# A hybrid decoder layer: key bias by DMA broadcast in place of six-row matmuls, and one new lane item per batch

## The chip, the core and the metric

The kernel runs on one core of a Trainium2 chip. The metric is the device time of one execution in microseconds (us). The core has a matrix engine (TensorE, PE in the profile; its weight loads are listed as PEld), a vector engine (VectorE, DVE), a scalar engine (ScalarE, ACT), GpSimd (POOL) and a queue engine (SyncE, SP). Each engine works through its own list of instructions in order; semaphores order them between engines.

## What is computed

One layer on 256 tokens of width 2048: a half-step feed-forward layer, a mixing layer of three attention groups, a second half-step feed-forward layer. All of it is float32 at the interface.

```python
x = x + 0.5 * swiglu(rms_norm(x, ffn1_norm), ffn1_gate, ffn1_up, ffn1_down)     # 2048 -> 5632 -> 2048
h = rms_norm(x, mix_norm); proj = h @ w_in
fq, fk, fv, f_logit, sq, sk, sv, mq = split(proj)
# A: forgetting attention, 6 heads of 128
log_f = log_sigmoid(f_logit + forget_bias); c = cumsum(log_f, axis=sequence)
s = (rms(fq) @ rms(fk).T) * scale + c[query] - c[key];  s = where(key <= query, s, NEG_INF)
out_a = softmax(s) @ fv
# B: windowed attention (128), 6 query heads on 2 key heads, distance penalty, sink logit
# C: 4 heads of attention into 256 memory rows
x = x + concat(out_a, out_b, out_c) @ w_out
x = x + 0.5 * swiglu(rms_norm(x, ffn2_norm), ffn2_gate, ffn2_up, ffn2_down)
```

The term that the change is about is `- c[key]`, one number for each key and each head, the same for all queries.

## The kernel before

**Projections and batches.** Every weight matrix goes through `project`. A batch is two slices of 128 rows of the weight, 512 columns wide (384 or 390 in parts of `w_in`). `load_w` issues its DMA on SP (tag `raw`, four buffers), ScalarE rounds it to a high part (`hi`, L205, three buffers), VectorE subtracts to get the low part (`lo`, L206, three buffers). `mm_rows` then runs three matmuls for each half of the tokens and each slice: high by high (L248), high activations by low weights (L249), low by high (L250). So a batch is 12 matmuls, and a projection of `w_in` has 8 batches. After each batch, `project` calls `lanes.tick()` once.

**Side work between batches.** Everything else is cut into stages, Python generators, which `Lanes` runs between the batches. A generator issues the instructions of a stage and yields the number of batches until its next stage. There are two kinds. Items given to `lanes.run` start at the next tick. Items given to `lanes.put` wait in a queue until those that they name have ended, and then until one of two lanes is free; each lane has its own PSUM tile (tags `l0`, `l1`). In `tick` both lanes may take a new item in the same call. `finish` calls `tick` without a projection batch until the named items have ended. The framework's planner may shift instructions on an engine among neighbours, but TensorE's order follows the code here.

**The mixing layer.** Its chunks of `w_in` come in the order mq, sqa (with the six forget logits), skv, sqb, fqa, fka, fqb, fkb, fva, fvb. After each, `heads_T` normalises the heads: squares of each head and token half on ScalarE (L396, 8 for four heads, 6 for three), reciprocal root on VectorE, scaled copies on ScalarE, transposes on TensorE back into the chunk's accumulator (L412), one copy out. Its stages lie 1, 3, 2 and 1 batches apart. The accumulators have two buffers.

`forget` makes the cumulative sums with small matmuls: `cq` for queries (128 partitions) and the negated `nck` for keys, on six partitions, one for each head (L481). It is put after sqa; in the profile `nck` is written during batch 7 of sqb.

`logits` handles a pair of heads: a windowed pair (w0, w2, w4) has four query-key matmuls (L495), two for each head, of 128 and 256 columns. A forgetting pair (f0, f2, f4) has before each of them a matmul that adds `nck` to every row of the tile: its weights are one sixth of `sel`, six rows of 128, a selector with ones in row h for head h (L493). Three batches later VectorE adds `cq` and the causal mask `cmask` from PSUM to SBUF (L507), takes the maxima, and three batches on ScalarE takes the exponentials. A float32 matmul is listed as two records in the profile.

f0 starts after batch 7 of fqb; f2 and f4 become ready together and start in both lanes after the last batch of fva.

## Time and profile before

| | |
|---|---|
| median of 3 runs | 1846.38 us (1846.11 to 1847.82) |
| the profiled execution | 1845.47 us |
| its span, first to last instruction | 1843.7 us |
| TensorE's mean granted clock in the span | 0.998 |
| busy: TensorE, weight loads, VectorE, ScalarE, GpSimd | 1829.9, 1538.8, 938.9, 846.4, 11.1 us |
| moved by DMA | 343.36 MB, mean 186 GB/s |

Busy is the time in which an engine works on an instruction, and matmuls overlap each other in these records, so the busy time of TensorE is no measure of how full it is; the distance between the starts of two matmuls is. Times in the rows are from the span's start. A granted clock of 1.00 is 2.4 GHz, 0.50 is 1.2 GHz. All rows come from the one profiled execution.

### The profile page before, as it was taken

How to read it: one execution, taken by the hardware profiler on the slowest of the kernel's cores; microseconds unless marked ns; L12 is line 12 of the kernel's file. 1: busy time of each engine (PE TensorE's matmuls, PEld its weight loads, DVE VectorE, ACT ScalarE, POOL GpSimd, SP SyncE). 2: the span in 40 equal slices, each digit the busy share in tenths (PEclk: the TensorE clock that was granted, in tenths of full speed). 3: DMA queues.
4: the chain of work that ended last, by engine and by line, in shares of the span. 5: the costliest groups of instructions: out<-in, count | busy, mean ns of one | idle time of the engine just before them, and what ended most of it. 6: DMA issues, size and time to landing. Idle time of an engine off the chain costs nothing.

```text
span 1843.7 us, 21918 instructions
## 1 busy us (share of the span) xinstructions
PE 1829.9 (99%) x8448; PEld 1538.8 (83%) x8448; DVE 938.9 (51%) x1121; ACT 846.4 (46%) x1148; POOL 11.1 (1%) x31
## 2 busy tenths in 40 slices
PE   8999999999999999999999999999999999999998
PEld 6888888888888888888998888888888888888887
DVE  5554544555445554645655455555555454544443
ACT  6444444444435443656665455444444444433332
POOL 2000000000000000000000000000000000000000
PEclk9999999999999999999999999999999999999999
DMA  7666666666656566565555556666666666666663
GB/s 231 192 189 189 193 186 191 191 188 192 187 191 206 194 210 193 176 175 147 161 143 145 179 181 189 192 186 192 188 190 193 184 192 187 192 194 204 206 204 128
DMA packets 182520, 343.36 MB, mean 186 GB/s; under 512 B 11088, under 2 KB 28048, under 8 KB 182416
## 3 DMA queue, kind: packets, MB, share of 16 engines
q1 hardware_dynamic: 180368, 339.04, 61.6%
q10 hardware_dynamic: 1696, 2.89, 0.4%
q8 instruction: 66, 1.08, 0.3%
q14 instruction: 38, 0.31, 0.1%
q0 software_dynamic: 352, 0.03, 0.0%
HBM read 339.83 MB, written 2.10 MB: 185 GB/s over the span
## 4 chain that ended last, share of the span: by engine, by line
PE 97%; DMA 1%; ACT 1%; DVE 1%; issue 0%; DVEq 0%; ACTq 0%
PE ga L248 4%; PE ga L250 4%; PE ga L249 4%; PE ua L248 4%; PE gb L248 4%; PE db L249 4%; PE db L250 4%; PE gb L249 4%; PE gb L250 4%; PE ub L248 4%; PE ua L249 4%; PE ua L250 4%; PE ub L249 4%; PE ub L250 4%; PE db L248 4%; PE da L249 4%
## 5 line engine op out<-in xcount | busy, mean ns | idle before, releaser
L206 DVE TENSOR_TENSOR lo_bu<-raw_bu,hi_bu 128x1024 fp32r<-128x1024 f32 x88 | 107.8, 1225 | 131.5 <-ACT hi_bu L205 131.5
L206 DVE TENSOR_TENSOR lo_au<-raw_au,hi_au 128x1024 fp32r<-128x1024 f32 x88 | 107.8, 1225 | 130.1 <-ACT hi_au L205 130.1
L206 DVE TENSOR_TENSOR lo_bd<-raw_bd,hi_bd 128x1024 fp32r<-128x1024 f32 x88 | 107.7, 1224 | 124.0 <-ACT hi_bd L205 124.0
L206 DVE TENSOR_TENSOR lo_ad<-raw_ad,hi_ad 128x1024 fp32r<-128x1024 f32 x88 | 107.8, 1224 | 119.5 <-ACT hi_ad L205 119.5
L205 ACT CAST hi_bd<-raw_bd 128x1024 fp32r<-128x1024 f32 x88 | 92.8, 1055 | 145.0 <-PE db L250 139.8
L206 DVE TENSOR_TENSOR lo_ag<-raw_ag,hi_ag 128x1024 fp32r<-128x1024 f32 x88 | 108.1, 1229 | 98.7 <-ACT hi_ag L205 98.7
L206 DVE TENSOR_TENSOR lo_bg<-raw_bg,hi_bg 128x1024 fp32r<-128x1024 f32 x88 | 107.7, 1223 | 99.2 <-ACT hi_bg L205 99.2
L205 ACT CAST hi_ad<-raw_ad 128x1024 fp32r<-128x1024 f32 x88 | 92.7, 1053 | 131.5 <-PE da L250 106.4
L205 ACT CAST hi_bg<-raw_bg 128x1024 fp32r<-128x1024 f32 x88 | 92.7, 1054 | 127.2 <-PE gb L250 68.3
L205 ACT CAST hi_ag<-raw_ag 128x1024 fp32r<-128x1024 f32 x88 | 92.7, 1054 | 122.5 <-PE ga L250 66.3
L205 ACT CAST hi_bu<-raw_bu 128x1024 fp32r<-128x1024 f32 x88 | 92.7, 1054 | 115.5 <-PE ub L250 79.0
L205 ACT CAST hi_au<-raw_au 128x1024 fp32r<-128x1024 f32 x88 | 92.7, 1054 | 115.3 <-PE ua L250 79.4
L248 PE MATMUL ga<-hi_ag,x0T 128*128 128x512 f32 x352 | 138.7, 394 | 0.0
L248 PE MATMUL gb<-hi_bg,x2T 128*128 128x512 f32 x352 | 137.9, 392 | 0.0
L250 PE MATMUL ga<-hi_ag,x0T 128*128 128x512 f32 x352 | 137.3, 390 | 0.0
L249 PE MATMUL ga<-lo_ag,x0T 128*128 128x512 f32 x352 | 137.3, 390 | 0.0
L248 PE MATMUL da<-hi_ad,hT_a 128*128 128x512 f32 x352 | 137.2, 390 | 0.0
L249 PE MATMUL da<-lo_ad,hT_a 128*128 128x512 f32 x352 | 137.1, 389 | 0.1
L250 PE MATMUL gb<-hi_bg,x2T 128*128 128x512 f32 x352 | 137.1, 389 | 0.0
L248 PE MATMUL ua<-hi_au,x0T 128*128 128x512 f32 x352 | 137.0, 389 | 0.0
L248 PE MATMUL db<-hi_bd,hT_b 128*128 128x512 f32 x352 | 137.0, 389 | 0.0
L249 PE MATMUL gb<-lo_bg,x2T 128*128 128x512 f32 x352 | 137.0, 389 | 0.0
(460 smaller groups left out, 3959.7 us busy)
## 6 DMA issues: line engine op xcount, KB each, us to landing
raw_ag<-in_ffn_gate_dram SPq DMA_DIRECT2D x88, 512.0 KB, 4.5
raw_au<-in_ffn_up_dram SPq DMA_DIRECT2D x88, 512.0 KB, 3.7
raw_ad<-in_ffn_down_dram SPq DMA_DIRECT2D x88, 512.0 KB, 4.7
raw_bg<-in_ffn_gate_dram SPq DMA_DIRECT2D x88, 512.0 KB, 4.3
raw_bu<-in_ffn_up_dram SPq DMA_DIRECT2D x88, 512.0 KB, 3.7
raw_bd<-in_ffn_down_dram SPq DMA_DIRECT2D x88, 512.0 KB, 4.6
raw_wo<-in_w_out_dram SPq DMA_DIRECT2D x16, 512.0 KB, 3.7
raw_mk<-in_w_mem_k_dram SPq DMA_DIRECT2D x8, 512.0 KB, 3.8
```

The source lines that it names most:

```text
L205: nc.scalar.copy(h, r)
L206: nc.vector.tensor_tensor(out=l, in0=r, in1=h.bitcast(F32), op=ALU.subtract)
L248: nc.tensor.matmul(acc[:, t, :w], hi, wh, start=first, stop=False)
L249: nc.tensor.matmul(acc[:, t, :w], hi, wl, start=False, stop=False)
L250: nc.tensor.matmul(acc[:, t, :w], lo, wh, start=False, stop=last)
```

## The change

Three edits. First, the negated key sums are no longer added by matmuls. `nck` becomes a corner of a tile `nck_all` of 128 partitions by six heads by 384 keys. GpSimd's queue writes the six rows to a DRAM scratch tile and reads them back to all 128 partitions (six rows of 1.5 KB, 9 KB for each partition). `add_mask`, an item of its own, waits six batches and then adds the causal mask to one head in each batch. The forgetting logits wait for it, and L507 takes `nck_all` where it took `cmask`. The six-row matmuls, `sel` and its two instructions go. Second, in `tick` only one of the lanes may take a new item. Third, `heads_T` squares one half of the tokens, waits a batch, squares the other, and waits two batches before the copies where it waited three.

```diff
     def tick(self):
         self.free = [i for i in self.free if self._step(i)]
+        started = False
         for n in range(2):
-            if self.lane[n] is None:
+            if self.lane[n] is None and not started:
                 for q in self.queue:
                     if all(d in self.done for d in q[2]):
                         self.queue.remove(q)
                         self.lane[n] = [q[0], q[1](f"l{n}"), 0]
+                        started = True
                         break
...
+    dpool = ctx.enter_context(tc.tile_pool(name="scratch", bufs=1, space=bass.MemoryType.DRAM))
...
-    sel = cpool.tile([6, 6, P], F32, name="sel")
...
-        nc.gpsimd.memset(sel, 0.0)
-        nc.gpsimd.affine_select(out=sel, in_=sel, compare_op=ALU.not_equal, fill=1.0, base=0,
-                                pattern=[[-1, 6], [0, P]], channel_multiplier=1)
...
                     nc.scalar.activation(junk, acc[:, t, cols(h)], AF.Square, scale=r[:, t:t + 1],
                                          accum_out=s[:, t, h:h + 1])
-            yield 1
+                yield 1
...
-            yield 3
+            yield 2
...
-        nck = mx.tile([6, 3 * P], F32, name="nck")
+        nck_all = mx.tile([P, 6, 3 * P], F32, name="nck_all")
+        nck = nck_all[0:6, 0, :]
+        nck_dram = dpool.tile([6, 3 * P], F32, name="nck_dram")
...
+        def add_mask():
+            yield 6
+            for h in range(6):
+                nc.vector.tensor_tensor(out=nck_all[:, h, :], in0=nck_all[:, h, :], in1=cmask, op=ALU.add)
+                yield 1
...
+            nc.gpsimd.dma_start(nck_dram, nck)
+            nc.gpsimd.dma_start(nck_all.rearrange("p h s -> p (h s)"),
+                              nck_dram.rearrange("h s -> (h s)")[None, :].to_broadcast([P, 6 * 3 * P]))
+            lanes.run("mask", add_mask())
...
                 for t, keys in enumerate((k[:, 0:P], k)):
-                    if fox:
-                        nc.tensor.matmul(sp[:, i, SEG[t]], sel[:, h0 + i, :], nck[:, SEG[t]], start=True,
-                                         stop=False)
-                    nc.tensor.matmul(sp[:, i, SEG[t]], q[:, t * P:(t + 1) * P], keys, start=not fox,
-                                     stop=True)
+                    nc.tensor.matmul(sp[:, i, SEG[t]], q[:, t * P:(t + 1) * P], keys, start=True, stop=True)
...
-                            in1=cmask[:, SEG[t]], op0=ALU.add, op1=ALU.add)
+                            in1=nck_all[:, h0 + i, SEG[t]], op0=ALU.add, op1=ALU.add)
...
-                lanes.put("f0", fox_logits(0), ("forget", "fqa", "fka"))
+                lanes.put("f0", fox_logits(0), ("mask", "fqa", "fka"))
...
-                    lanes.put(f"f{h}", fox_logits(h), ("forget", "fqa", "fka", "fqb", "fkb"))
+                    lanes.put(f"f{h}", fox_logits(h), ("mask", "fqa", "fka", "fqb", "fkb"))
```

## Rows read from the trace of the kernel before

**Rows 1.** The page, first section: engine, busy us, share, instructions.
```profile
PE 1829.9 (99%) x8448; PEld 1538.8 (83%) x8448; DVE 938.9 (51%) x1121; ACT 846.4 (46%) x1148; POOL 11.1 (1%) x31
```

**Rows 2.** TensorE's waits, 100 to 1840: us in total, times, longest.
```profile
PE sqa L249 <- DVE lo_sqa L206: 0.5, 1, 0.5
```

**Rows 3.** Windows: stretch, its us, busy us by engine, PEclk, DMA share, GB/s.
```profile
885.00:890.00 5.00, 5.00 (x31) 4.90 (x30) 3.48 (x12) 4.37 (x15) 0.00 (x0) 1.00 0.17 48
985.00:992.00 7.00, 7.00 (x32) 4.36 (x30) 2.87 (x7) 2.14 (x4) 0.00 (x0) 1.00 0.57 164
992.00:999.00 7.00, 7.00 (x19) 5.07 (x19) 2.95 (x9) 2.12 (x9) 0.00 (x0) 0.51 0.01 2
```

**Rows 4.** TensorE's timeline around f0: start us, duration us, what, idle before.
```profile
944.63 0.34 PE L250 MATMUL fqb<-hi_fqb,x1T 128*128 128x384 f32 x1
944.90 0.48 PE L493 MATMUL s_f<-nck,sel 6*128 6x128 f32 x2
...
949.16 0.33 PE L249 MATMUL fkb<-lo_fkb,x1T 128*128 128x384 f32 x1
```

**Rows 5.** TensorE's timeline around w0, and six ordinary steps after it.
```profile
884.77 0.33 PE L250 MATMUL sqb<-hi_sqb,x1T 128*128 128x384 f32 x1
884.94 1.47 PE L495 MATMUL s_w<-qkv 128*128 128x128 f32 x8
...
886.43 0.34 PE L249 MATMUL fqa<-lo_fqa,x1T 128*128 128x384 f32 x1
...
887.47 0.33 PE L249 MATMUL fqa<-lo_fqa,x1T 128*128 128x384 f32 x1
```

**Rows 6.** TensorE's timeline around f2 and f4.
```profile
986.09 0.34 PE L250 MATMUL fva<-hi_fva,x1T 128*128 128x384 f32 x1
...
991.99 1.22 PE L495 MATMUL s_f<-qkv 128*128 128x256 f32 x2
...
996.39 0.88 PE L248 MATMUL fvb<-hi_fvb,x1T 128*128 128x384 f32 x1
...
998.92 0.34 PE L249 MATMUL fvb<-lo_fvb,x1T 128*128 128x384 f32 x1
```

**Rows 7.** TensorE's timeline around v0 with v2, and around v4.
```profile
1029.14 0.39 PE L250 MATMUL wo<-hi_wo0e,mixT 128*128 128x512 f32 x1
...
1032.22 0.40 PE L249 MATMUL wo<-lo_wo1e,mixT 128*128 128x512 f32 x1
...
1039.94 0.39 PE L250 MATMUL wo<-hi_wo1e,mixT 128*128 128x512 f32 x1
...
1041.70 0.40 PE L249 MATMUL wo<-lo_wo1e,mixT 128*128 128x512 f32 x1
```

**Rows 8.** Timelines of ScalarE and TensorE at the squares of `mq`.
```profile
816.49 0.37 ACT L396 ACTIVATE junkh<-mq,y_x 128x128 f32<-128x128 f32 x1 [1.87 <-PE mq L250]
...
819.25 2.36 ACT L205 CAST hi_sqa<-raw_sqa 128x780 fp32r<-128x780 f32 x3
...
821.38 0.44 PE L249 MATMUL sqa<-lo_sqa,x1T 128*128 128x390 f32 x1 [0.48 <-DVE lo_sqa L206]
```

**Rows 9.** DMA issues: tile, issuing queue, count, KB each, median us to landing.
```profile
raw_fqa<-in_w_in_dram SPq DMA_DIRECT2D x8, 384.0 KB, 4.2
x_sb<-in_x_dram ACTq DMA_DIRECT2D x3, 512.0 KB, 11.5
graw<-in_ffn_norm_dram POOLq DMA_DIRECT2D x1, 8.0 KB, 6.7
```

**Rows 10.** Timelines of VectorE and TensorE from the key bias to the last `fqa` batch.
```profile
883.01 0.54 DVE L481 TENSOR_SCALAR nck<-cps 6x384 f32<-6x384 f32 x1
886.52 1.02 DVE L512 SCALAR_TENSOR_TENSOR ss_w<-dist,s_w 128x384 f32<-128x384 f32 x2 [2.98 <-PE s_w L495]
...
897.77 0.96 DVE L206 TENSOR_TENSOR lo_fqa<-raw_fqa,hi_fqa 128x768 fp32r<-128x768 f32 x1 [0.41 <-ACT hi_fqa L205]
...
901.66 0.34 PE L249 MATMUL fqa<-lo_fqa,x1T 128*128 128x384 f32 x1
```

## The prediction

> **What bounds the kernel now.** I read the page first: TensorE is busy for 1829.9 us of a span of 1843.7 us, at a mean granted clock of 0.998 [rows 1]. Next the waits: between the start and the end TensorE waits once, for 0.5 us, on a `lo` tile of batch `sqa` [rows 2]. So an edit is worth what it takes from TensorE's own queue, or what new wait it puts there; ScalarE, VectorE and the DMA queues have time left. Then the windows around the forgetting attention's logits: from 985 to 992 the engine is busy 7.00 of 7.00 us at clock 1.00, from 992 to 999 busy 7.00 of 7.00 us at 0.51, which is the lower level of 1.2 GHz, and 19 matmuls go through where 32 went before [rows 3]. The clock fell there with no idle time ahead of it. Last, the timeline of TensorE by start times [rows 4 to 7]. A matmul's own duration overlaps the next one's, so I price an interlude between projection matmuls as the distance of two ordinary starts on either side of it, and compare interludes by these distances.
>
> **The six-row matmuls.** The change removes four per pair of heads, for three pairs. The pair f0 runs alone and at full clock: from the last L250 before it (944.63) to the L249 after it (949.16) there are 4.53 us, with four six-row and four query-key matmuls (two records each) in between [rows 4]. The windowed pair w0 has the same four query-key matmuls, 8 records of 128 and 256 columns, and no six-row ones: from 884.77 to 886.43, 1.66 us [rows 5]. After the change a forgetting pair has the form of w0. Saved for f0: 4.53 - 1.66 = 2.87 us.
>
> Pairs f2 and f4 start in one batch and stand back to back. From L250 at 986.09 to the eighth projection matmul after them, L249 at 998.92, there are 12.83 us [rows 6]. Six ordinary steps of 384 columns lie between the second and the eighth; w0's are 887.47 - 886.43 = 1.04 us, so 0.173 each [rows 5]. That leaves 12.83 - 1.04 = 11.79 us to the second one. After the change f4 starts one batch later, so there are two interludes like w0's: 1.66 for the first, and 1.66 less two ordinary steps, 1.31, for the second. Saved: 11.79 - 1.66 - 1.31 = 8.82 us. Of this the clock is 11.79 - 4.53 - (4.53 - 0.35) = 3.08 us, the rest is again 2.87 per pair. Sum of both places: 11.69 us.
>
> That counts the clock as staying up. My reason: it fell at 991.99, inside the longest run of such work in the trace, 10 us from the L250 at 986.09 to the L248 at 996.39 [rows 6], and not in f0's run of 4 us with the same matmuls [rows 4]; after the change such a run is w0's, 8 records in 1.47 us [rows 5], with a whole batch of 12 projection matmuls between f2 and f4.
>
> The row also says why so much goes: f0 costs 4.18 us beyond its ordinary steps and w0 1.31, so adding as many six-row matmuls more than triples the cost. The Trainium skill (TensorE: Matmul & The Clock Gate, section Why this matters for your kernels) says that a single matmul of few rows takes the same time as one of 128; by that each six-row matmul would cost what its query-key partner costs in w0, and the three pairs would be worth 3 x 1.31 = 3.9 us in place of 8.6. The trace disagrees where the two kinds alternate; I go by the rows, and keep the other as a rival.
>
> **One new item per lane round.** Pairs that now start together (memory and mixing transposes, the memory heads m0 and m2, f2 and f4, v0 and v2) start one batch apart. That makes more, shorter interludes of the same work. Their price: v0 and v2 in one interlude take 3.08 us from L250 to L249, v4 alone takes 1.76 [rows 7]. Two ordinary steps of 512 columns are in both (0.173 x 512/384 = 0.23 each), so the second pair adds 1.32 and a lone pair costs 1.76 - 0.46 = 1.30. Splitting is free within 0.02 us, for about ten places under 0.2 us in all: taken as nothing. The places at which the program waits for the lanes to empty come out the same: counted through the yields, v4 is put and ends in the same batches as before, f0 starts in the same batch, and no round without a projection batch is added.
>
> **Head squares in two parts.** `heads_T` now spreads its squares over two batches and shortens the later pause by one, so copies, transposes and the release of the accumulator keep their batch. The only wait of TensorE comes from here: eight squares of `mq` hold ScalarE from 816.49 to 819.25, the casts queued behind them come late, and the matmul at 821.38 waits 0.48 us for `lo_sqa` [rows 8, 2]. With four squares ahead of the first cast this cast ends about 1.4 us earlier, more than the wait. I take -0.5 us; the other end is 0, if the planner orders ScalarE another way.
>
> **The mask through DRAM.** `forget` issues two DMAs on POOL's queue, which has nothing else by then: 9 KB out, then 1152 KB in, the second after the first has landed. Six batches later VectorE adds the causal mask to six tiles of 128x384, and f0 to f4 wait for that. Neither transfer nor wait is in the trace, so bounds. The key bias is there at 883.01 + 0.54 = 883.55 [rows 10]. A small DMA of POOL's queue landed 6.7 us after issue at the start of the program; that serves for the first. For the second, a 384 KB weight tile lands in 4.2 us [rows 9]; three times that is 12.6 us, though part of each 4.2 does not grow with size. Landing by these: 902.9. With both DMAs of the small kind and nothing for the bytes: 897.0. Upper end: the 512 KB pieces of `x` took 11.5 us while everything else was being loaded [rows 9]; 2.25 times that is 25.9, landing at 916. I take a value near the lower end, because the DMA engines are only 0.17 busy from 885 to 890 [rows 3], just where the transfer falls.
>
> Who waits: VectorE is in order, so the first add, if the data isn't there, holds the `lo` tile behind it, and that holds TensorE. The add stands just ahead of the last `lo_fqa`, which before starts at 897.77 after 0.41 us of idle time, and is done at 898.73; TensorE first reads it at 901.66 [rows 10]. So a landing up to 897.4 costs nothing at all. From there the lead of 901.66 - 898.73 = 2.9 us, less the first add's 0.5, covers a landing up to some 900; beyond, each us late is a us of the span. The three landings give 0, 3 and 16 us. I take 0; a gain is excluded, since nothing waited for here goes away. The six adds themselves are 6 x 0.51 = 3.1 us (half of the x2 row of the same shape, 1.02) [rows 10], one per batch of 2.1 us, on an engine with idle time there. The logits' own VectorE work keeps its shape: the masked key bias replaces the mask as an operand. The six-row selector's two POOL instructions at the start go, beside other work: nothing.
>
> A rule against this part is that of the Trainium skill (DMA: Bandwidth & Descriptors, section SWDGE vs HWDGE vs iDMA): POOL's DMAs have their descriptors written to SBUF by GpSimd, which VectorE locks out in its two-port mode. Here VectorE sits idle for 2.98 us just after the key bias is made [rows 10], so the first DMA is not held; no run so far shows the second, which would come in a busy stretch, and the delay would be inside the bounds above.
>
> **Sum.** -11.69 - 0.5 + 0 = -12.2 us. The profiled execution took 1845.47 us: 1833.3. The median of the three runs is 0.9 us above it; taking that over gives 1834.2 us.
>
> **The rivals.**
> B, the clock falls all the same, at the shorter logits or at another interlude. For: it fell in a stretch with no idle time, so what matters is not only waiting. Against: 7 us at half clock are all that a mean of 0.998 has room for, so no other interlude lost it, m0 and m2 together and the transposes included. It gives back 3.1 us: 1837.3.
> C, only the six-row matmuls' bare share goes, 3 x 1.31 = 3.9 us, and the query-key matmuls stay as dear as they are next to them; with the clock and the ScalarE wait 7.5 us: 1838.9. Against: w0 has just this form.
> D, the broadcast lands some 3 us late (middle bound): TensorE waits for `lo_fqa`, 1837.2, up to 1840 for 6 us late.
> E, on the other side: the broadcast is slow like the loads at the start, all 128 partitions reading one 9 KB row. VectorE stands at the first add, TensorE behind it. It eats the whole gain when it lands after 900 + 12.2 = 912; at the far bound, 916, it is 16 us late and the kernel is at 1850.2, slower by a bare 0.2%. Against: the idle DMA engines.
>
> **How the numbers follow.** Forecast 0.72; B 0.12; C 0.03; D 0.08; E 0.05. A measurement can tell some 0.2%, 3.7 us, from no change, so faster means under 1842.7. Forecast, B, C and D all are: 0.95, less 0.02 for a late landing between D and E. Within 0.2%: 0.03; slower 0.04, for E at its far end and beyond. The range goes from 1833.0 (the profile's own sum, less a little) to 1838.0, which takes in B and most of D: 0.85 to 0.9 by the cases.
>
> **What would show it.** TensorE's interludes f0, f2 and f4 each like w0's 1.66 us; granted clock 1.00 from 985 on, with no half-clock stretch before the end; no wait on `lo_sqa`; VectorE's first add without idle time before it, and no TensorE wait for `lo_fqa` or `lo_fka`. I am wrong if TensorE shows waits of several us after the key bias, if the clock drops in another place, or if a forgetting pair costs clearly more than a windowed one.

## The result

Five executions of the changed kernel take 1833.47 us in the median (1832.94 to 1834.20), five of the kernel before, beside them, 1846.38 us (1845.80 to 1847.82). The ratio is 0.9926, 95% interval 0.9915 to 0.9937. Put on 1846.38 us that is 1832.7 us, with 1830.7 to 1834.7 by the interval. The two medians by themselves differ by a little less, 12.9 us in place of 13.7. The forecast was 1834.2 us, a gain of 12.2, with a range from 1833.0 to 1838.0: the direction and the main mechanism came out, the gain is 0.7 us larger than forecast by the medians and 1.5 by the ratio, and the time by the ratio lies just under the low end.

The profiled execution took 1832.94 us, its span is 1831.2 us. In the changed file the helpers stand two lines higher: L246, L247, L248 are the three projection matmuls (L248, L249, L250 before), L203 and L204 the rounding and the subtraction, L394 the squares, L503 the query-key matmuls, L487 the key bias, L468 the mask additions, L490 and L491 the two DMAs. First the page's totals, which answer to [rows 1]; 24 matmul records are gone, four six-row matmuls of two records for three pairs:

```profile
PE 1818.1 (99%) x8424; PEld 1532.2 (84%) x8424; DVE 941.8 (51%) x1127; ACT 846.1 (46%) x1148; POOL 11.6 (1%) x31
```

TensorE's waits (waited for: us in total, times, longest), one of the start and that of [rows 2]. Past the start there is no other, and it has stayed:

```profile
PE tp_x L219 <- DMA x_sb<-in_x_dram: 3.2, 1, 3.2
...
PE sqa L247 <- DVE lo_sqa L204: 0.5, 1, 0.5
```

Windows (columns as in [rows 3]), the same stretches as there. The half clock has gone; from 992 to 999, 42 matmuls go through where 19 did, and from 885 to 890, with the broadcast under way, the DMA share is 0.41 where it was 0.17:

```profile
885.00:890.00 5.00, 5.00 (x31) 4.95 (x30) 4.44 (x16) 4.50 (x12) 0.58 (x1) 1.00 0.41 115
985.00:992.00 7.00, 7.00 (x43) 6.90 (x42) 6.84 (x17) 5.14 (x19) 0.00 (x0) 1.00 0.42 114
992.00:999.00 7.00, 7.00 (x42) 7.00 (x42) 4.55 (x11) 3.52 (x5) 0.00 (x0) 1.00 0.70 222
```

TensorE's timeline around f0, f2 and f4, the rows that answer to [rows 4] and [rows 6]:

```profile
943.67 0.33 PE L248 MATMUL fqb<-hi_fqb,x1T 128*128 128x384 f32 x1
943.84 1.47 PE L503 MATMUL s_f<-qkv 128*128 128x128 f32 x8
...
945.33 0.34 PE L247 MATMUL fkb<-lo_fkb,x1T 128*128 128x384 f32 x1
...
982.26 0.33 PE L248 MATMUL fva<-hi_fva,x1T 128*128 128x384 f32 x1
...
983.92 0.34 PE L247 MATMUL fvb<-lo_fvb,x1T 128*128 128x384 f32 x1
...
985.66 0.33 PE L248 MATMUL fvb<-hi_fvb,x1T 128*128 128x384 f32 x1
...
987.31 0.34 PE L247 MATMUL fvb<-lo_fvb,x1T 128*128 128x384 f32 x1
```

Each of the three is 1.66 us from the ordinary start before it to the one behind it (945.33 - 943.67, 983.92 - 982.26, 987.31 - 985.66 with the last digit rounded), w0's figure of [rows 5], and a whole batch lies between f2 and f4.

Where the 12.5 us of span went can be read from the start of the first projection matmul of a chunk in either timeline:

| first matmul of | before | after | difference |
|---|---|---|---|
| gate of the first feed-forward layer | 10.23 | 8.94 | -1.29 |
| mk (memory keys) | 746.49 | 745.40 | -1.09 |
| fqa | 886.07 | 885.10 | -0.97 |
| fkb (f0 lies before it) | 948.79 | 944.96 | -3.83 |
| w_out (f2 and f4 lie before it) | 1014.36 | 1001.70 | -12.66 |
| end | 1843.75 | 1831.19 | -12.55 |

From fqa to w_out, 12.66 - 0.97 = 11.69 us: to the hundredth what the prediction summed for this stretch. One us came from the very start and was not forecast; the squares brought nothing.

The start is chance, as it differs as much between executions of one file. The first instruction of TensorE that waits for `x` starts at 8.33 in the profile before and at 7.04 after; in two more profiles of the kernel before, further down, it starts at 7.21 and 7.92.

### The profile page after: what moved, and what is told of

Read it like the earlier page. It is cut to its first block, busy times and chain, and to the rows that moved or that the text cites. A ratio compares the mean times of both kernels' runs of the same rounds, so it can differ in the third digit from the quotient of the medians.

```text
span 1831.2 us, 21875 instructions
## 1 busy us (share of the span) xinstructions
PE 1818.1 (99%) x8424; PEld 1532.2 (84%) x8424; DVE 941.8 (51%) x1127; ACT 846.1 (46%) x1148; POOL 11.6 (1%) x31
## 4 chain that ended last, share of the span: by engine, by line
PE 99%; DMA 0%; ACT 0%; DVE 0%; issue 0%; DVEq 0%; ACTq 0%
PE ga L246 4%; PE ga L248 4%; PE ga L247 4%; PE ua L246 4%; PE da L248 4%; PE gb L248 4%; PE db L248 4%; PE gb L247 4%; PE gb L246 4%; PE da L247 4%; PE ub L247 4%; PE ua L248 4%; PE da L246 4%; PE ua L247 4%; PE ub L248 4%; PE ub L246 4%
## 5 line engine op out<-in xcount | busy, mean ns | idle before, releaser
L204 DVE TENSOR_TENSOR lo_bu<-raw_bu,hi_bu 128x1024 fp32r<-128x1024 f32 x88 | 107.8, 1226 | 131.5 <-ACT hi_bu L203 131.5
L204 DVE TENSOR_TENSOR lo_au<-raw_au,hi_au 128x1024 fp32r<-128x1024 f32 x88 | 107.8, 1225 | 130.0 <-ACT hi_au L203 130.0
L204 DVE TENSOR_TENSOR lo_bd<-raw_bd,hi_bd 128x1024 fp32r<-128x1024 f32 x88 | 107.8, 1225 | 123.9 <-ACT hi_bd L203 123.9
L204 DVE TENSOR_TENSOR lo_ad<-raw_ad,hi_ad 128x1024 fp32r<-128x1024 f32 x88 | 107.8, 1225 | 116.7 <-ACT hi_ad L203 116.7
L203 ACT CAST hi_bd<-raw_bd 128x1024 fp32r<-128x1024 f32 x88 | 92.8, 1055 | 145.0 <-PE db L248 139.8
L204 DVE TENSOR_TENSOR lo_ag<-raw_ag,hi_ag 128x1024 fp32r<-128x1024 f32 x88 | 107.9, 1226 | 99.2 <-ACT hi_ag L203 99.2
L204 DVE TENSOR_TENSOR lo_bg<-raw_bg,hi_bg 128x1024 fp32r<-128x1024 f32 x88 | 107.7, 1224 | 99.1 <-ACT hi_bg L203 99.1
L203 ACT CAST hi_ad<-raw_ad 128x1024 fp32r<-128x1024 f32 x88 | 92.7, 1053 | 129.1 <-PE da L248 104.7
L203 ACT CAST hi_bg<-raw_bg 128x1024 fp32r<-128x1024 f32 x88 | 92.7, 1054 | 127.2 <-PE gb L248 68.3
L203 ACT CAST hi_ag<-raw_ag 128x1024 fp32r<-128x1024 f32 x88 | 92.8, 1054 | 121.3 <-PE ga L248 66.7
L203 ACT CAST hi_bu<-raw_bu 128x1024 fp32r<-128x1024 f32 x88 | 92.7, 1054 | 115.5 <-PE ub L248 79.0
L203 ACT CAST hi_au<-raw_au 128x1024 fp32r<-128x1024 f32 x88 | 92.7, 1054 | 115.3 <-PE ua L248 79.4
L246 PE MATMUL ga<-hi_ag,x0T 128*128 128x512 f32 x352 | 138.5, 393 | 0.0
L246 PE MATMUL gb<-hi_bg,x2T 128*128 128x512 f32 x352 | 137.9, 392 | 0.0
L246 PE MATMUL da<-hi_ad,hT_a 128*128 128x512 f32 x352 | 137.4, 390 | 0.0
L248 PE MATMUL ga<-hi_ag,x0T 128*128 128x512 f32 x352 | 137.4, 390 | 0.0
L247 PE MATMUL ga<-lo_ag,x0T 128*128 128x512 f32 x352 | 137.2, 390 | 0.0
L248 PE MATMUL gb<-hi_bg,x2T 128*128 128x512 f32 x352 | 137.1, 389 | 0.0
L247 PE MATMUL da<-lo_ad,hT_a 128*128 128x512 f32 x352 | 137.0, 389 | 0.0
L246 PE MATMUL ua<-hi_au,x0T 128*128 128x512 f32 x352 | 137.0, 389 | 0.0
L246 PE MATMUL db<-hi_bd,hT_b 128*128 128x512 f32 x352 | 137.0, 389 | 0.0
L248 PE MATMUL da<-hi_ad,hT_a 128*128 128x512 f32 x352 | 137.0, 389 | 0.0
```

Source lines behind the costliest of these rows:

```text
L203: nc.scalar.copy(h, r)
L204: nc.vector.tensor_tensor(out=l, in0=r, in1=h.bitcast(F32), op=ALU.subtract)
L246: nc.tensor.matmul(acc[:, t, :w], hi, wh, start=first, stop=False)
L247: nc.tensor.matmul(acc[:, t, :w], hi, wl, start=False, stop=False)
L248: nc.tensor.matmul(acc[:, t, :w], lo, wh, start=False, stop=last)
```

## Which edit carries it: one part at a time

Theory: the gain is the key bias alone, through two effects, the six-row matmuls' own time and the clock. Rival: the edit that puts pairs one batch apart keeps the clock up by itself, and the squares bring half a us.

**Key bias alone.** The changed kernel with the old `tick` and the old `heads_T`:

```diff
         for n in range(2):
-            if self.lane[n] is None and not started:
+            if self.lane[n] is None:
...
-                yield 1
...
+            yield 1
...
-            yield 2
+            yield 3
```

> The key bias through DRAM alone; the lanes and the squares as before, so f2 and f4 again start in the same batch, back to back, now without six-row matmuls. Theory (the clock fell because of the six-row matmuls in a long run): f2 with f4 takes 1.31 us less than two ordinary interludes, the granted clock stays 1.00, and the kernel gains the whole 11.7 us over the kernel before, within 0.5 us of all three edits. Rival (two pairs in one batch are enough for the clock to fall, and the lane rule is what kept it up): a half-clock stretch after f2 and f4, 3.1 us dearer, a gain of 8.6 us.

Measured: 1833.81 us (1832.91 to 1834.03, five runs), ratio 0.9924 (0.9911 to 0.9936) to the kernel before, which beside it took 1847.52 us in the median (1843.52 to 1849.44). f2 and f4 stand back to back here. TensorE's timeline (helpers another two lines higher):

```profile
983.46 0.33 PE L246 MATMUL fva<-hi_fva,x1T 128*128 128x384 f32 x1
983.63 2.78 PE L501 MATMUL s_f<-qkv 128*128 128x128 f32 x16
...
986.42 0.34 PE L245 MATMUL fvb<-lo_fvb,x1T 128*128 128x384 f32 x1
```

and its window around them:

```profile
980.00:1005.00 25.00, 25.00 (x147) 24.37 (x146) 16.37 (x32) 14.96 (x31) 0.00 (x0) 1.00 0.64 197
```

Both pairs together take 986.42 - 983.46 - 0.35 = 2.61 us, twice 1.31, at full clock. From the first matmul of fkb to the first of w_out there are 56.74 us, exactly as in the changed kernel. The key bias is the whole gain; the other two edits add nothing that the runs can tell.

**The lane rule alone**, on the kernel before:

```diff
+        started = False
         for n in range(2):
-            if self.lane[n] is None:
+            if self.lane[n] is None and not started:
...
                         self.lane[n] = [q[0], q[1](f"l{n}"), 0]
+                        started = True
```

> The lane rule alone; the six-row matmuls stay, but f4 starts one batch of 12 projection matmuls after f2. Theory (the clock fell in a run of 10 us; a run of 4 us as in f0 doesn't bring it down): the clock stays 1.00, a gain of 3.1 us over the kernel before, to some 1843.3. Rival (two such runs with 2.1 us between them are enough): a half-clock stretch near f4 or after it, a gain of 0 to 1 us. The start of the program, where x's transposes now stand one batch apart: no difference by the theory.

Measured: 1843.25 us (1840.74 to 1846.08, seven runs), ratio 0.9979 (0.9968 to 0.9989). That the time falls a little is as expected, the reason for it is not. Windows of the profiled execution (1846.08 us, the longest of the seven), around f0 and around f2 and f4:

```profile
940.00:965.00 25.00, 25.00 (x124) 22.54 (x124) 12.57 (x34) 13.15 (x36) 0.00 (x0) 0.86 0.47 112
943.00:947.00 4.00, 4.00 (x18) 2.60 (x17) 0.59 (x4) 2.92 (x13) 0.00 (x0) 0.97 0.56 147
947.00:953.00 6.00, 6.00 (x19) 5.08 (x19) 3.72 (x14) 0.22 (x1) 0.00 (x0) 0.50 0.23 65
980.00:1005.00 25.00, 25.00 (x123) 21.10 (x122) 13.45 (x26) 11.33 (x28) 0.00 (x0) 0.93 0.41 115
```

A mean of 0.86 over 25 us is 0.14 x 25 x 2 = 7 us at half clock, and 0.93 is another 3.5 us. Both stretches begin inside a single pair, with the engine busy throughout: f0's matmuls start at 943.70 and end at 948.90, and the clock falls just before 947; f4's run from 994.62 to 999.55, and the clock is 1.00 up to about 998 and then falls. The prediction's reason for a clock that stays up, that f0's run of 4 us had not brought it down [rows 4], is refuted: it can.

The same file once more:

> The lane rule alone, a second profile. In the first one the clock fell at f0 (6.8 us) and at f4 (3.4 us). If a six-row run of 4 us brings it down by chance of when it falls, this profile has a stretch at f0, at f2 or at f4 or at none, other than the first; if it is fixed by the order of the work, the same two stretches. The kernel before, whose f0 is the same, has shown none at f0 in two profiles.

Measured: one execution of 1841.80 us, span 1840.1 us, and no fall at any of the three pairs; the windows:

```profile
940.00:965.00 25.00, 25.00 (x143) 23.00 (x142) 14.00 (x35) 14.21 (x38) 0.00 (x0) 1.00 0.58 134
980.00:1005.00 25.00, 25.00 (x132) 21.40 (x131) 14.21 (x30) 11.44 (x27) 0.00 (x0) 1.00 0.47 142
```

So in one and the same file a pair's run of 4 us can bring the clock down or leave it up; what decides it these runs do not show. This execution gives a useful measure, the old matmuls without a fall: 62.48 us from the first matmul of fkb to the first of w_out. In the profile before these are 1014.36 - 948.79 = 65.57, so the clock cost 3.09 there; the prediction had 3.08.

**The squares alone**, on the kernel before:

```diff
                                          accum_out=s[:, t, h:h + 1])
-            yield 1
+                yield 1
...
-            yield 3
+            yield 2
```

> The head squares in two parts alone. What the trace after shows (all eight squares of mq in one piece ahead of the casts): the planner puts the halves together again, TensorE waits 0.5 us for lo_sqa as before, and the time is that of the kernel before within 0.3 us. Rival (the edit needs the others' order to be ineffective): the halves are apart and the 0.5 us are gained.

Measured: 1847.04 us (1844.66 to 1849.75, 11 runs), ratio 0.9997 (0.9989 to 1.0006). The wait for `lo_sqa` is there as before. Why is plain in ScalarE's timeline of the changed kernel:

```profile
810.02 0.85 ACT L203 CAST hi_sqa<-raw_sqa 128x780 fp32r<-128x780 f32 x1 [1.67 <-PE mq L248]
812.74 0.85 ACT L203 CAST hi_sqa<-raw_sqa 128x780 fp32r<-128x780 f32 x1 [1.87 <-PE mq L248]
815.47 0.37 ACT L394 ACTIVATE junkh<-mq,y_x 128x128 f32<-128x128 f32 x1 [1.87 <-PE mq L248]
...
818.23 2.36 ACT L203 CAST hi_sqa<-raw_sqa 128x780 fp32r<-128x780 f32 x3
```

The first square waits for the last matmul of mq, and the casts of sqa's batches 0 and 1 are long done by then. The cast that comes late is that of batch 2, and the program issues it behind both halves of the squares, since these are only one batch apart. So all eight squares still run in one piece ahead of it, to 818.23.

## The squares, put far enough apart

To see whether the wait can go at all, the halves were put two batches apart in the changed kernel, and the pause behind them cut to one:

```diff
                                          accum_out=s[:, t, h:h + 1])
-                yield 1
+                yield 2 - t
...
-            yield 2
+            yield 1
```

> The changed kernel with the second half of the head squares two batches after the first in place of one, and one batch less before the copies. In the profiles so far ScalarE has done the casts of sqa's batches 0 and 1 before mq's accumulator is ready, so both halves, one batch apart, still stand ahead of the late cast, that of batch 2. Theory: two batches apart, the cast of batch 2 comes between the halves, ends some 1.4 us earlier, and the wait of 0.5 us for lo_sqa is gone; the time is that of the changed kernel less 0.6 us, which the timing can hardly tell. Rival (the planner groups the squares whatever their batch): eight in one piece again and the wait stays.

Measured: 1835.13 us (1834.27 to 1835.86, four runs), ratio 0.9929 (0.9913 to 0.9946). ScalarE now has a cast between the halves, and the wait for `lo_sqa` is gone:

```profile
817.58 0.37 ACT L394 ACTIVATE junkh<-mq,y_x 128x128 f32<-128x128 f32 x1
...
817.92 0.86 ACT L203 CAST hi_sqa<-raw_sqa 128x780 fp32r<-128x780 f32 x1
818.65 0.39 ACT L394 ACTIVATE junkh<-mq,y_x 128x128 f32<-128x128 f32 x1
```

The squares' part is won: from the first matmul of sqa to that of fqa there are 69.07 us, 0.77 less than the 69.84 of the changed kernel. But the whole gains nothing, because a longer wait has come up at the mask: from fqa to fka 20.97 us in place of 18.62. The first addition of the mask, in VectorE's timeline, and TensorE's wait behind it:

```profile
895.24 0.56 DVE L468 TENSOR_TENSOR nck_all<-nck_all,cmask 128x384 f32<-128x384 f32 x1 [2.93 <-DMA nck_all<-nck_dram]
```

```profile
PE fqa L247 <- DVE lo_fqa L204: 1.8, 2, 1.6
```

The broadcast took 8.3 us from issue to landing here and 6.3 in the changed kernel; why, these runs do not say. They show how little room the mask has, which the next section takes up.

## What the broadcast costs, and what it costs when it is late

The DMA issues of the changed kernel (KB, and us from issue to landing), then the first addition and its neighbours on VectorE:

```profile
nck_all<-nck_dram POOLq DMA_DIRECT2D x1, 1152.0 KB, 6.3
nck_dram<-nck_all POOLq DMA_DIRECT2D x1, 9.0 KB, 3.2
```

```profile
893.08 0.56 DVE L468 TENSOR_TENSOR nck_all<-nck_all,cmask 128x384 f32<-128x384 f32 x1 [0.58 <-DMA nck_all<-nck_dram]
893.64 0.55 DVE L468 TENSOR_TENSOR nck_all<-nck_all,cmask 128x384 f32<-128x384 f32 x1
894.18 0.96 DVE L204 TENSOR_TENSOR lo_fqa<-raw_fqa,hi_fqa 128x768 fp32r<-128x768 f32 x1
...
896.79 0.95 DVE L204 TENSOR_TENSOR lo_fqa<-raw_fqa,hi_fqa 128x768 fp32r<-128x768 f32 x1
...
898.38 0.95 DVE L204 TENSOR_TENSOR lo_fqa<-raw_fqa,hi_fqa 128x768 fp32r<-128x768 f32 x1
```

and TensorE's first use of the `lo` tile of 896.79:

```profile
897.94 0.34 PE L247 MATMUL fqa<-lo_fqa,x1T 128*128 128x384 f32 x1
```

The data landed at 893.0, 4 us ahead of the earliest time in the prediction, 897.0; one us of that is the earlier start of the whole program. And the first addition stands ahead of three more `lo_fqa` tiles, not just ahead of the last one (898.38): in the program the six additions are one batch apart, here most of them stand close together, so the planner had moved them. The prediction would have let a landing up to 897.4 pass free. With the place that the addition really has, it would not have been free. VectorE has no gap from 893.08 on, the `lo` tile of 896.79 is done at 897.74, and TensorE reads it at 897.94: 0.2 us of room. Two kernels with the addition in the same place bear this out. Counted from the first matmul of fqa, it starts at 7.98 us in the changed kernel. With the key bias alone it starts at 8.38, 0.4 later, and from fqa to fka there are 18.99 us in place of 18.62. With the squares apart it starts at 9.84, 1.86 later, with three additions ahead of the next `lo` tile in place of two (0.55 us more), and fqa to fka takes 2.35 us longer. The prediction's 897.0 is 10.93 counted this way, 2.95 later than here, and would have cost nearly 3 us in this place.

Rival D was then made real: two more trips of the 9 KB through DRAM ahead of the broadcast.

```diff
             nc.gpsimd.dma_start(nck_dram, nck)
+            src = nck_dram
+            for trip in range(2):
+                dst = dpool.tile([6, 3 * P], F32, name=f"nck_trip{trip}")
+                nc.gpsimd.dma_start(dst, src)
+                src = dst
             nc.gpsimd.dma_start(nck_all.rearrange("p h s -> p (h s)"),
-                              nck_dram.rearrange("h s -> (h s)")[None, :].to_broadcast([P, 6 * 3 * P]))
+                              src.rearrange("h s -> (h s)")[None, :].to_broadcast([P, 6 * 3 * P]))
```

> The changed kernel with two more copies from DRAM to DRAM between the write of the key bias and the broadcast, each issued after the one before has landed. In the changed kernel the broadcast landed at 893.0, 6.3 us after issue, and the first add stands right behind it. By the prediction's lead, landing up to some 900 is covered. Each trip should cost 3 to 4 us, so the broadcast lands between 899 and 901: VectorE waits some 6 us at the first add unless the planner moves it, and TensorE waits 0 to 1 us. Rival (the lead is shorter than reckoned, as weight tiles behind the add come late as well): TensorE waits 3 us or more, up to the whole delay of 7.

Measured: 1839.61 us (1838.14 to 1840.76, four runs), ratio 0.9959 (0.9944 to 0.9974); 6.1 us above the changed kernel by the medians. VectorE's rows, TensorE's row and the windows around it:

```profile
902.78 1.03 DVE L468 TENSOR_TENSOR nck_all<-nck_all,cmask 128x384 f32<-128x384 f32 x2 [5.67 <-DMA nck_all<-nck_trip]
903.72 0.95 DVE L204 TENSOR_TENSOR lo_fqa<-raw_fqa,hi_fqa 128x768 fp32r<-128x768 f32 x1
```

```profile
904.73 0.69 PE L247 MATMUL fqa<-lo_fqa,x1T 128*128 128x384 f32 x1 [3.17 <-DVE lo_fqa L204]
```

```profile
901.00:905.00 4.00, 0.83 (x6) 0.58 (x5) 2.22 (x4) 1.51 (x2) 0.00 (x0) 0.83 0.47 175
905.00:910.00 5.00, 5.00 (x17) 4.82 (x18) 3.29 (x6) 1.47 (x9) 0.00 (x0) 0.50 0.62 169
910.00:915.00 5.00, 5.00 (x29) 4.88 (x29) 4.07 (x12) 3.23 (x12) 0.00 (x0) 0.95 0.19 69
```

The trips took 2.0 and 4.6 us and the broadcast 8.2, so the data landed at 902.7, later than expected. Here the addition does stand ahead of the last `lo_fqa`, where the prediction had put it, and the wait of 3.17 us is about what its reckoning gives: some 2.7 us past 900, and 0.5 for a second addition ahead of the tile. During the wait the granted clock fell to the lower level, and it came back at about 910.5 (0.05 x 5 x 2 = 0.5 us of the third window). From the matmul at 904.73 on that is some 5.8 us of work at half speed, 2.9 us lost: 6.1 in all, the figure of the medians. So the prediction's price for this rival, "each us late is a us of the span", left out the part that the clock takes, about half here. This fall is the kind that the Trainium skill describes (TensorE: Matmul & The Clock Gate, section Why this matters for your kernels): the clock drops after gaps in which TensorE has nothing to do. The trace agrees: the clock fell in the wait of 3.17 us, while the one of 1.6 us in the kernel with the squares apart left it at 1.00. The fall of [rows 3], with the engine busy 7.00 of 7.00 us, is not of that kind.

## Why a six-row matmul costs so much

Theory: the cost is not in the matmul but in the change of row count between neighbours, since the next weights aren't loaded ahead across it. Rival: any matmul put into this interlude costs what the six-row ones did. In the kernel before, the six-row operands were given 128 rows, zero below the sixth; the result is the same.

```diff
-    sel = cpool.tile([6, 6, P], F32, name="sel")
+    sel = cpool.tile([P, 6, P], F32, name="sel")
...
-        nck = mx.tile([6, 3 * P], F32, name="nck")
+        nck = mx.tile([P, 3 * P], F32, name="nck")
...
+            nc.gpsimd.memset(nck, 0.0)
...
-            nc.vector.tensor_scalar(out=nck,
+            nc.vector.tensor_scalar(out=nck[0:6, :],
```

> The kernel before with the key bias matmul on 128 rows in place of six: selector and key bias are filled with zeros below, so it adds the same. The number and the order of matmuls stay. Theory (a six-row matmul is dear because it alternates with 128-row ones and the weight load then isn't hidden): f0's interlude falls from 4.18 us beyond the ordinary steps to 2 x 1.31 = 2.6, f2 with f4 to 5.2, and the clock stays 1.00; with the clock's 3.1 us a gain of 3 x 1.56 + 3.1 = 7.8 us. Rival (it is the accumulation of two matmuls on one output that is dear, whatever the rows): 4.18 stays, the clock falls as before, no gain.

Measured: 1837.99 us (1836.79 to 1838.41, four runs), ratio 0.9950 (0.9933 to 0.9966). The same number of matmuls on the same number of columns, and f0 takes 947.67 - 944.70 = 2.97 us where it took 4.53 [rows 4]:

```profile
944.70 0.34 PE L250 MATMUL fqb<-hi_fqb,x1T 128*128 128x384 f32 x1
944.87 0.38 PE L494 MATMUL s_f<-nck,sel 128*128 128x128 f32 x2
...
947.67 0.34 PE L249 MATMUL fkb<-lo_fkb,x1T 128*128 128x384 f32 x1
```

**Half as many changes.** Again the kernel before with its six rows, but for each half of the tokens the six-row matmuls of both heads first and then the two query-key matmuls: four changes of row count in a pair in place of eight.

```diff
-            for i in range(2):
-                q, k = qT(h0 + i), kT(h0 + i)
-                for t, keys in enumerate((k[:, 0:P], k)):
-                    if fox:
+            for t in range(NT):
+                if fox:
+                    for i in range(2):
                         nc.tensor.matmul(sp[:, i, SEG[t]], sel[:, h0 + i, :], nck[:, SEG[t]], start=True,
                                          stop=False)
-                    nc.tensor.matmul(sp[:, i, SEG[t]], q[:, t * P:(t + 1) * P], keys, start=not fox,
-                                     stop=True)
+                for i in range(2):
+                    q, k = qT(h0 + i), kT(h0 + i)
+                    nc.tensor.matmul(sp[:, i, SEG[t]], q[:, t * P:(t + 1) * P], (k[:, 0:P], k)[t],
+                                     start=not fox, stop=True)
```

> The kernel before with the same six-row matmuls in another order: for each token half both heads' six-row matmuls, then both query-key ones. So the rows change 4 times in a pair of heads and not 8. Theory (each change costs): the excess of a pair over 8 plain matmuls, 4.18 - 2.62 = 1.56 us, is about halved, f0 at some 3.4; the run of f2 and f4 shortens by 1.6 us. Rival (a six-row matmul costs more by itself): 4.18 stays. The clock: falls by either, as the run is still over 6 us of such work; a stay would say that the run must be longer than that.

Measured: 1840.88 us (1840.42 to 1842.48, five runs), ratio 0.9967 (0.9954 to 0.9980). f0 takes 948.72 - 944.97 = 3.75 us. TensorE's timeline, then the weight loads under it:

```profile
944.97 0.34 PE L250 MATMUL fqb<-hi_fqb,x1T 128*128 128x384 f32 x1
945.24 0.71 PE L492 MATMUL s_f<-nck,sel 6*128 6x128 f32 x4
945.88 0.71 PE L496 MATMUL s_f<-qkv 128*128 128x128 f32 x4
...
948.72 0.33 PE L249 MATMUL fkb<-lo_fkb,x1T 128*128 128x384 f32 x1
```

```profile
944.80 0.19 PEld L250 LDWEIGHTS fqb<-hi_fqb,x1T 128*128 128x128 f32 x1
945.24 0.52 PEld L492 LDWEIGHTS s_f<-nck,sel 6*128 6x128 f32 x4 [0.25 <-issue]
```

The weights of the ordinary matmul at 944.97 are loaded from 944.80, while the matmul before it runs. At the change of row count the load begins only at 945.24, in the same 0.01 us as its matmul. With 128 rows throughout it began at 944.70 for the matmul at 944.87:

```profile
944.70 0.36 PEld L494 LDWEIGHTS s_f<-nck,sel 128*128 128x128 f32 x2
```

The three pairs line up. Beyond the two ordinary steps of 0.35 us, f0 costs 2.62 us with no change of row count, 3.40 with four, 4.18 with eight: 0.78 / 4 = 0.195 and 1.56 / 8 = 0.195 us for each change. The rest of what these two gained is put down to the clock, which stayed at 1.00 from 980 to 1005 in both: by the medians they gained 9.6 and 6.7 us against 1847.55 us of the kernel before beside them, of which 3 x 1.56 = 4.7 and 3 x 0.78 = 2.3 us are the changes, so 4.9 and 4.3 us are left. So the prediction's 2.87 us for a pair is 4 matmuls that cost as much as their partners, 1.31, and eight changes, 1.56. The Trainium skill says (TensorE: Matmul & The Clock Gate, section LDWEIGHTS (loading the stationary operand)) that loading few rows takes as long as loading 128. The trace agrees on the duration of a load, 0.18 us in the median for six rows and 0.19 for 128 in the kernel before; where it starts is the matter here.

## The clock

The two kernels above were also made for the clock. If a long run of float32 matmuls brings it down, then 128 rows, run as long, must do it; if it is the six-row matmuls in alternation, they must not. Two more matmuls with zeros, on 128 rows, were put behind each of the key bias's:

```diff
                         nc.tensor.matmul(sp[:, i, SEG[t]], sel[:, h0 + i, :], nck[:, SEG[t]], start=True,
                                          stop=False)
+                        for _ in range(2):
+                            nc.tensor.matmul(sp[:, i, SEG[t]], sel[:, h0 + i, :], zero[:, SEG[t]],
+                                             start=False, stop=False)
```

> As the kernel with 128 rows, and each key bias matmul is followed by two more that add zeros, so a pair has 16 float32 matmuls and f2 with f4 a run of some 10.5 us, as long as the six-row run of the kernel before. Theory (six rows are what brings the clock down): the clock stays 1.00 through it. Rival (any long run of float32 matmuls does it): a half-clock stretch near the end of f4. The time is longer than that of the kernel with 128 rows by 3 x 2.6 = 7.9 us with the clock up.

Measured: one execution of 1845.25 us, 7.3 above the median of the kernel with 128 rows where 7.9 was expected. f2 and f4 now make a run of 10.5 us, as long as that of [rows 6] at full clock and half clock together, and the clock stays up:

```profile
980.00:1005.00 25.00, 25.00 (x152) 24.14 (x151) 13.43 (x30) 11.11 (x26) 0.00 (x0) 1.00 0.40 112
```

With four changes of row count in a pair, where the expectation had the clock fall, it stayed up too, in a run of 6.8 us; the same file once more:

> The kernel with half as many switches between six-row and 128-row matmuls, a second profile. In the first one the clock stayed at 1.00 through a run of 6.8 us. If the denser order is what keeps it up, it stays up again; if the first was chance, a half-clock stretch at f2 and f4 here.

Measured: 1840.08 us, and again no fall:

```profile
980.00:1005.00 25.00, 25.00 (x142) 22.95 (x141) 15.10 (x31) 11.96 (x27) 0.00 (x0) 1.00 0.53 158
```

All six timed executions of this file have a mean granted clock of 0.999 or 1.000, so here it was not one lucky profile.

How much does the fall cost in the kernel before? It was profiled twice more.

> The kernel before, unchanged, for a second profile. The trace after has the first transposes of x at 7.04 us, 1.29 us earlier than before. If that is chance in when the pieces of x land, this profile's start differs from the first one's by up to a us or so, and the rest is the same from the first projection matmul on. If the change did it, this profile has 8.3 us again. The half-clock stretch should be at the same place, f4.

> The kernel before, a third profile, for the size of the clock's share. The first profile has 6.8 us at half clock at f2 and f4, the second 10.2. Theory: 6.8 or 10.2 us at this place in every execution, so 3.1 to 5 us of its time, and the prediction's 3.08 was the low end. Rival: it can stay up or fall at f0 as well, then the length is 0 or over 13 us.

Measured: 1846.57 us (1845.32 to 1848.73, ten runs), ratio 0.9999 (0.9989 to 1.0008), for the first, one execution of 1846.04 us for the second. The window of the first, 0.80 (the second has 0.80 as well), and that of the profile before:

```profile
980.00:1005.00 25.00, 25.00 (x105) 20.08 (x104) 11.77 (x28) 10.41 (x25) 0.00 (x0) 0.80 0.35 99
```

```profile
980.00:1005.00 25.00, 25.00 (x115) 20.39 (x113) 12.57 (x28) 10.79 (x26) 0.00 (x0) 0.86 0.40 111
```

0.20 x 25 x 2 = 10 us at half clock where the profile before had 0.14 x 25 x 2 = 7. From the first matmul of fkb to the first of w_out they take 67.15 and 67.14 us, 4.7 us more than the 62.48 without a fall; the kernel with the squares alone has 67.13. And the 38 executions of the kernel before that were timed beside the experiments fall into groups by their mean granted clock:

| mean granted clock | executions | mean span, us |
|---|---|---|
| 0.996 | 20 | 1846.8 |
| 0.997 | 8 | 1845.1 |
| 0.998 | 9 | 1843.5 |
| 0.999 | 1 | 1841.8 |

The span goes with the clock. The profile before, at 0.998 and 1843.7 us, belongs to the quarter that lost least. Against the 1840.1 us of the execution without a fall, the mean of all 38, 1845.5 us, gives an estimate of 5.4 us lost to the clock in an average execution. It rests on one execution of the kernel with the lane rule, whose start can be a us off by chance. What the change itself gained gives another: 12.9 us by the medians and 13.7 by the ratio, less 8.61 for the matmuls, leave 4.3 to 5.1 us.

## The prediction, point by point

**What bounds the kernel: right.** Between the start and the end every us of the result is one that TensorE's queue lost or gained.

**The six-row matmuls: right.** 2.87 us for a pair, three times, 8.61. f0, f2 and f4 came out at w0's 1.66, and from fqa to w_out this pair of profiles gives the 11.69 that was summed. Rival C is out: the partners of six-row matmuls were dear because of the changes of row count, which go with them.

**The clock: the effect right, its size wrong, its reason in part.** The step of the prediction that failed is this term of its sum, "Of this the clock is ... 3.08 us". It was read from the one profiled execution, and that was one of the mild ones. Three other profiles of the same order of work lose 4.7, and the measured gain, with 8.61 for the matmuls and nothing for the squares, leaves 4.3 to 5.1 us for the clock on average. As a reading of that one profile it was exact (3.09); as a term for the time of an average execution it was 1.2 to 2.0 us short, against which the squares' 0.5 went the other way. The last step of the sum did not make it good: it carried the 0.9 us between the profile and the median over to the kernel after whole. Some of this stays after the change, whose median lies 0.5 us above its own profile with the clock up in both; the rest is of a size with what the clock takes from one execution to the next, but the clock of those three executions is not on record. The reason given for a clock that stays up was wrong as well, since f0's 4 us can bring it down; what the runs show is that it stayed up wherever the alternation of six and 128 rows was gone, or half as dense. Rival B, a fall in spite of the change, did not come: 1.00 in all windows.

**The squares: wrong, 0 in place of -0.5.** The step that failed is "with four squares ahead of the first cast this cast ends about 1.4 us earlier". The first casts were done before the squares began; the late one is that of batch 2, and it is issued behind both halves. The other end named there, 0, is what came. Two batches apart, the halves do win 0.77 us at that place.

**The lane rule: right on its price, 0.** Distances with and without it are the same, 56.74 us. It had a use that the prediction did not see, on the kernel before alone, where it splits the long run of six-row matmuls and saves 0.2%; with the key bias gone from TensorE there is nothing left of it.

**The mask through DRAM: 0 is right, by two errors that cancel.** The landing came 4 us earlier than the lower bound (3.2 and 6.3 us for the two transfers, where the bound had 6.7 for each, and a start one us earlier), and the first addition stands ahead of three `lo_fqa` tiles, not one. With the right place and the foreseen landing the price would have been near 3 us, rival D. That rival's price in turn lacked the clock: 3.2 us of waiting cost 6.1. Rival E is far off.

**The start: not priced.** The first wait for `x` ends a us earlier or later between executions of the same file; it gave this profile 1.3 us, of which 1.0 is left at fqa.

**The range: too narrow below.** Its low end was the sum of one profile less a little. With 8.6 us for the matmuls and 3.1 to 6.7 for the clock (the last is the group at 0.996, 1846.8 - 1840.1), against the median of 1846.4 us, it should have reached down to about 1831.

## What to carry to other kernels

Price a small matmul by the distance of ordinary starts around it, and see whether its row count differs from its neighbours': the change, not the matmul, was more than half the cost here, and padding to full rows or grouping takes much of it back with the same number of matmuls. A clock loss read from one execution is a sample: compare the profile's mean clock with that of the other timed executions before a term is taken from it, and ask whether a difference between profile and median can outlive the change before it is carried over. A transfer that is just in time should be judged by the place that its consumer got on its engine in the finished order, and a wait on TensorE priced with the clock if it drops it: 3.2 us cost about double here, 1.6 us did not.

## What the runs showed of the hardware

- The granted clock fell from 2.4 to 1.2 GHz with TensorE busy throughout, inside runs of alternating six-row and 128-row float32 matmuls: in four profiles out of four where f2 and f4 made one long run, and in one of two where each pair stood alone, in f0 and in f4; f0 alone left it up in the other five. It did not fall in a run of the same matmuls with half the changes of row count (two profiles, 6.8 us), nor in 10.5 us of 128-row float32 matmuls (one). What it reacts to, the changes, the gaps between loads or the few rows, isn't settled, nor why the stretches at half clock differ (3.5, 7 and 10 us).
- A change of row count between neighbouring float32 matmuls, from 128 to six or back, cost 0.195 us; the next weight load did not start ahead of it, as it did between equal row counts.
- The broadcast of 9 KB to 1152 KB over 128 partitions took 6.3 to 8.3 us on GpSimd's queue, the 9 KB out 3.1 to 3.4.
